# A fused multiply and GELU on one core: the first 4096 columns stored by the ACT queue while the last y load runs

## The chip, the cores, the metric

One core of one Trainium2 chip. The metric is the device time of one execution in microseconds (us); a median is given with its lowest and highest run. The kernels with no repeated timing (two, marked below) have one run each.

## The reference

```python
# x, y: float32, 1024 x 4096
z = x * y
out = 0.5 * z * (1 + tanh(sqrt(2 / pi) * (z + 0.044715 * z ** 3)))
```

Two arrays of 16.78 MB are read and one is written, 50.33 MB in all. Nothing is used twice.

## The kernel before

Each of the 128 partitions holds 8 rows of the matrix, that is 32768 columns of float32 (128 KB), contiguous in the main memory. x stays in a buffer of full size and is overwritten by the product and then by the result. y passes through a ring of half that size.

```python
X_LOADS = [(0, 16384), (16384, 32768)]
Y_LOADS = [(0, 16384, 0), (16384, 24576, 0), (24576, 32768, 8192)]   # from, to, place in the ring
STEP = 4096
STORES = [(0, 16384), (16384, 32768)]
# ... (set-up cut)
_hoist(nc, [load_x(0).ins, load_y(0).ins])       # issued at the very start, on SyncE
load_x(1)
for i in (1, 2):                                 # the ring must be free first
    nc.sync.wait_ge(sem_mul, (Y_LOADS[i][1] - Y_LOADS[1][0]) // STEP)
    load_y(i)

n = 0
for i, (a, b, r) in enumerate(Y_LOADS):
    # ... (wait for the x load of these columns, cut)
    nc.vector.wait_ge(sem_y[i], 16)
    for c in range(a, b, STEP):
        nc.vector.tensor_mul(...).then_inc(sem_mul, 1)          # xs = xs * ys
        n += 1
        nc.scalar.wait_ge(sem_mul, n)
        nc.scalar.activation(..., func=GELU).then_inc(sem_act, 1)   # xs = gelu(xs)

for i, (a, b) in enumerate(STORES):
    nc.sync.wait_ge(sem_act, b // STEP)
    nc.sync.dma_start(out=out_r[:, a:b], in_=xs[:, a:b]).then_inc(sem_o[i], 16)
for i in range(len(STORES)):
    nc.sync.wait_ge(sem_o[i], 16)
```

All transfers of the kernel are issued by SyncE, in this order: x0, y0, x1, y1, y2, store 0, store 1. "y2" is the last y load, "the last store" is that of columns 16384 to 32768.

## Time and profile before

| | before |
|---|---|
| time, first 3 runs | 121.03 us (120.79 to 121.08) |
| span of the profiled run | 119.5 us |
| VectorE, ScalarE busy | 35.0 us, 30.2 us |
| DMA engines busy | 98.5% of the span |
| last store: issued, then time to landing | 93.32 us, 26.1 us |

The page's groups give the length of one instruction (the number after the busy time, in ns), and the view of the tensor `out_dram` gives the time from issue to landing of its two stores.

```profile
L87 DVE TENSOR_TENSOR xs<-xs,ys 128x4096 f32<-128x4096 f32 x8 | 35.0, 4421 | 54.7 <-DMA ys<-in_y_dram 54.7
L94 ACT ACTIVATE xs<-xs 128x4096 f32<-128x4096 f32 x8 | 28.9, 3617 | 61.1 <-DVE xs L87 61.1
...
DMA to landing us min/median/max: 26.1/31.9/37.7
```

Both engines idle far longer than they work, and VectorE waits for nothing but y. The two stores are of the same size, yet one takes 26.1 and the other 37.7 us to land: the difference is time spent standing in the queue. The trace also has one record for each row that a DMA engine moves ("packet records" below); they are not a view of the page and are quoted as worked out from the trace. The records carry no engine number: 16 chains were put together by matching each start to the end before it, and each comes to the same 3.15 MB, but for a few of the smallest rows. The excess of a row is its duration less the median for its size. The "dip" is the mean excess per engine around the place where stores first follow loads.

### The profile page before, as it was taken

What the parts mean: (1) busy time and instruction counts of PE and PEld (TensorE: products, weight loads), DVE (VectorE), ACT (ScalarE), POOL (GpSimd) and SP (SyncE); (2) the same over time, 40 slices, a digit from 0 to 9 for tenths busy, and PEclk for the clock granted to TensorE, in tenths of its full rate; (3) what the DMA queues carried; (4) which work ended last, traced back from release to release, by engine and by line L of the source; (5) the groups of instructions that cost most, each with busy time, mean ns of one, the idle gap of its engine ahead of it and who ended that gap; (6) DMA issues with size and microseconds to landing.
All of it is one profiled execution on the core that took longest, in us unless ns stands there. A gap on an engine that the chain in (4) does not pass through costs nothing.

```text
span 119.5 us, 68 instructions
## 1 busy us (share of the span) xinstructions
DVE 35.0 (29%) x8; ACT 30.2 (25%) x9; POOL 0.2 (0%) x4
## 2 busy tenths in 40 slices
DVE  0000000000000199999600049959990000000000
ACT  3000000000000006797780000977479200000000
POOL 0000000000000000000000000000000000000000
DMA  9889888998899889988898989998899888988890
GB/s 351 351 373 680 351 351 351 636 417 351 351 636 417 351 351 526 526 351 351 351 526 351 504 373 482 395 526 351 351 395 658 351 351 351 702 351 351 351 680 22
DMA packets 1008, 50.33 MB, mean 421 GB/s; under 512 B 112, under 2 KB 112, under 8 KB 112
## 3 DMA queue, kind: packets, MB, share of 16 engines
q1 hardware_dynamic: 1008, 50.33, 98.5%
HBM read 33.55 MB, written 16.78 MB: 421 GB/s over the span
## 4 chain that ended last, share of the span: by engine, by line
DMA 53%; DVE 22%; ACT 3%; SPq 0%; issue 0%; DVEq 0%
DMA ys<-in_y_dram 53%; DVE xs L87 22%; ACT xs L94 3%; SPq L66 0%; DVEq L85 0%
## 5 line engine op out<-in xcount | busy, mean ns | idle before, releaser
L87 DVE TENSOR_TENSOR xs<-xs,ys 128x4096 f32<-128x4096 f32 x8 | 35.0, 4421 | 54.7 <-DMA ys<-in_y_dram 54.7
L94 ACT ACTIVATE xs<-xs 128x4096 f32<-128x4096 f32 x8 | 28.9, 3617 | 61.1 <-DVE xs L87 61.1
L94 ACT ACT_TABLE_LOAD x1 | 1.3, 1283 | 1.9 <-PEq L54 1.9
L120 POOL MEMSET const-bfloat16-1.0<- 128x1 bf16 x1 | 0.1, 102 | 0.0
L120 POOL MEMSET const-uint8-127<- 128x1 uint8 x1 | 0.1, 102 | 0.0
L120 POOL MEMSET const-float32-1.0<- 128x1 f32 x1 | 0.1, 99 | 0.0
L120 POOL MEMSET const-float32-0.0<- 128x1 f32 x1 | 0.1, 98 | 0.2 <-issue 0.2
## 6 DMA issues: line engine op xcount, KB each, us to landing
ys<-in_y_dram SPq DMA_DIRECT2D x2, 4096.0 KB, 21.1
xs<-in_x_dram SPq DMA_DIRECT2D x2, 40.3
out_dram<-xs SPq DMA_DIRECT2D x2, 31.9
ys<-in_y_dram SPq DMA_DIRECT2D x1, 40.8
```

The costliest lines, as they stand in the source:

```text
L87: nc.vector.tensor_mul(out=xs[:, c : c + STEP], in0=xs[:, c : c + STEP], in1=ys[:, r + c - a : r + c - a + STEP],).then_inc(sem_mul, 1)
L94: nc.scalar.activation(out=xs[:, c : c + STEP], in_=xs[:, c : c + STEP], func=GELU).then_inc(sem_act, 1)
L120: nc = _bacc.Bacc("TRN2", target_bir_lowering=False, num_devices=1)
```

## The change

The intent: begin to store before the loads are done, from a second queue, so that stores don't have to wait at the end of the line of loads.

```diff
-STORES = [(0, 16384), (16384, 32768)]
+STORES = [(0, 4096), (4096, 16384), (16384, 32768)]
...
+    def store(engine, i):
+        a, b = STORES[i]
+        engine.wait_ge(sem_act, b // STEP)
+        engine.dma_start(out=out_r[:, a:b], in_=xs[:, a:b]).then_inc(sem_o[i], 16)
...
             nc.scalar.wait_ge(sem_mul, n)
+            if c == Y_LOADS[1][0]:
+                store(nc.scalar, 0)
             nc.scalar.activation(
...
-    for i, (a, b) in enumerate(STORES):
-        nc.sync.wait_ge(sem_act, b // STEP)
-        nc.sync.dma_start(out=out_r[:, a:b], in_=xs[:, a:b]).then_inc(sem_o[i], 16)
+    store(nc.sync, 1)
+    store(nc.sync, 2)
```

## The prediction

> **What bounds the kernel now.** I read the page's head and its DMA rows first, because 33.55 MB in and 16.78 MB out with eight multiplies and eight activations looks like a copy with some arithmetic on the side.
>
> ```profile
> span 119.5 us, 68 instructions
> DVE 35.0 (29%) x8; ACT 30.2 (25%) x9; POOL 0.2 (0%) x4
> DMA  9889888998899889988898989998899888988890
> DMA packets 1008, 50.33 MB, mean 421 GB/s; under 512 B 112, under 2 KB 112, under 8 KB 112
> q1 hardware_dynamic: 1008, 50.33, 98.5%
> ```
>
> VectorE and ScalarE are busy under a third of the span; the 16 DMA engines are busy in every slice, 98.5% of the span, all on one queue. Next the chain of waits and the waits of the SyncE queue:
>
> ```profile
> DMA 53%; DVE 22%; ACT 3%; SPq 0%; issue 0%; DVEq 0%
> SPq L70 <- DVE xs L87: 56.2, 2, 47.9
> SPq L100 <- ACT xs L94: 33.8, 2, 30.5
> SPq L102 <- DMA out_dram<-xs: 25.8, 1, 25.8
> ```
>
> The chain ends at the issue of the second store and gives VectorE 22%. Taken literally it says that an earlier multiply would end the program earlier. That has to be checked against the time order, since a store that is issued may still stand in line:
>
> ```profile
> 58.80 0.33 SPq L70 DMA_DIRECT2D ys<-in_y_dram  x1
> 62.45 31.22 SPq L100 DMA_DIRECT2D out_dram<-xs  x2
> 74.92 3.62 ACT L94 ACTIVATE xs<-xs 128x4096 f32<-128x4096 f32 x1 [12.51 <-DVE xs L87]
> 80.88 8.76 DVE L87 TENSOR_TENSOR xs<-xs,ys 128x4096 f32<-128x4096 f32 x2 [1.66 <-DMA ys<-in_y_dram]
> 89.68 3.62 ACT L94 ACTIVATE xs<-xs 128x4096 f32<-128x4096 f32 x1 [0.72 <-DVE xs L87]
> ...
> 93.32 0.34 SPq L100 DMA_DIRECT2D out_dram<-xs  x1
> ```
>
> The first store is issued at 62.45 and the view of its tensor gives 37.7 us to landing, so it lands at 100.1, although 8.39 MB at 433 GB/s is only 19.4 us: it waits behind the y loads until about 80. The second is issued at 93.32, while the first is still moving; its data can start only at about 99.3. So it has 99.3 - 93.32 = 6.0 us of slack, about 5 after start-up latency (the first load of the program is issued at 0.00 and its first packet starts at 1.01). The 22% of VectorE is under cover of the queue. Stretches cut at these points:
>
> ```profile
> 60.00:76.80 16.80, 6.33 (x2) 4.29 (x2) 0.00 (x0) 1.00 0.98 425
> 76.80:80.00 3.20, 2.43 (x1) 2.48 (x2) 0.00 (x0) 1.00 1.07 369
> 80.00:99.30 19.30, 8.76 (x2) 10.11 (x3) 0.00 (x0) 1.00 0.99 431
> 99.30:118.50 19.20, 0.00 (x0) 0.00 (x0) 0.00 (x0) 1.00 1.00 433
> ```
>
> The columns end with the DMA share and GB/s. Loads alone reach 425, stores alone 431 to 433, and only 76.8 to 80.0, the last two rows of the last y load on each engine, dips to 369. The packet records of the trace (one record is one contiguous row of a partition) say the same per engine: the 640 packets of 64 KB have a median of 2.418 us, 27.1 GB/s, and the 256 of 32 KB 1.213 us. Fifteen of the 16 engines have no gap over 0.05 us between their first packet and the last. Each engine moves 3.146 MB, and 3.146 MB / 27.1 GB/s = 116.1 us. With 1.0 us before the first packet, 0.8 us more in that first packet, about 0.7 us in the dip, 0.2 us of slight slowing between 50 and 60, and some 0.5 us from the last packet to the end, this is 119.3 of the 119.5 us. The kernel is bound by bytes through the DMA engines, and all that a reordering can win back is the dip and what lies at the ends.
>
> **What the Trainium skill says.** First, the page "DMA: Bandwidth & Descriptors", section "Issuing engines are not separate DMA queues": transfers issued by ScalarE and SyncE end on the same 16 engines and interleave, and a second issuer saves only issue time. The issue rows here are 0.33 to 0.43 us each and hide behind a full queue, so there is nothing to save. Second, the same page, "Queues, rings and completion order": each engine goes round-robin between the rows that have work, at packet granularity. The trace of before has one queue only, so it can't confirm this. Third, "Where 436 GB/s comes from": 435 GB/s is given as the ceiling of the ports; the 433 GB/s of the last stretch agrees, and loads and stores reach the same figure here. Fourth, the page "Perfetto Trace Analysis", section "DMA Optimizations": loads on one issuing engine and stores on another may make sense. That is the change's intent; no run yet shows it.
>
> **The change part by part.**
> 1. Bytes: none added or removed. Rows of the first store go from one of 64 KB to one of 16 KB and one of 48 KB. From the two medians, fixed cost of a packet is 2 x 1.213 - 2.418 = 0.008 us. An engine has 8 partitions, so 8 x 0.008 = 0.064 us, and one more semaphore packet of 0.009 us: +0.07 us, on the path that sets the end.
> 2. ScalarE issues the small store once multiply 5 is done, at about 74.9. By the issue rows it costs it some 0.4 us, so the activation that starts at 74.92 starts near 75.3 and ends near 78.9. The next one starts at 79.26 because of multiply 6, so this delay is absorbed: 0.
> 3. The small store's data can start near 75.9 (issue to first packet 1.0 us). At that moment an engine is in its sixth y row of eight (75.63 to 76.84 on the engine that I followed), with two left. In turn with rows of 16 KB (estimate 0.61 us each by half of 1.213), they land about 2 x 0.61 = 1.2 us later: the last y load lands at 82.0 in place of 80.8.
> 4. The last two multiplies, the last activation and the second big store all move by this 1.2 us: issue at about 94.5, first data possible near 95.5. The bytes queued ahead of it are the same as before, so its turn comes at 99.3 + 0.07. Hidden, with almost 4 us left. Cost: 0.
> 5. The remaining five or six small rows alternate with 48 KB rows of the first SyncE store. The order changes, the sum doesn't.
> 6. The SyncE wait for a third store semaphore is satisfied long before the last one: 0.
>
> Sum: +0.07 us, plus or minus what the dip does.
>
> **The rivals.**
> *A bubble before the last store.* If the ScalarE row were served wholly ahead of the y rows, the y load would land 8 x 0.61 = 4.9 us later, at 85.7; 8.77 us of multiplies, 3.62 us of activation and 1.0 us of latency later the last store could start at 99.1. Its turn is at 99.3. Even this worst order just fits, and would cost 0 to 0.5 us: at most 121.6.
> *Switching between loads and stores costs.* The dip stands right before the one place where the program turns from loads to stores. If the turn causes it (0.7 us each), an alternation of two or three y rows with small rows makes three to five turns: +1.4 to +2.8 us, 122.4 to 123.8. Against it: the dip starts two rows before the turn, on all engines at the same time, which looks as much like a slow moment of the memory as a cost of the turn. One trace can't tell.
> *Loads and stores overlap.* If an engine could read for a store while it writes for a load, the 2.1 MB store would be partly free. Only the two or three y rows that remain can be its partners: at most about 2.4 us, 118.6. Against it: loads and stores both sit at the same 27.1 GB/s per engine, as if one common data path set it.
> *The dip goes.* If the second queue fills what stalls there, 0.7 us is won: 120.4.
>
> **Range and chances.** Center: 121.03 + 0.07 = 121.1 us. Before itself spread from 120.79 to 121.08. Down to 120.2 covers the dip gone and good luck; up to 122.2 covers one or two more turns. 2% is 2.42 us: faster needs full overlap of all that can overlap, 3%; slower needs nearly the full turn cost or a bubble that I don't see, 6%; within 2%, 91%.
>
> **What would show it.** A second DMA queue with about 2.1 MB on the page, and a DMA share near 98%; the wait of VectorE for the last y load longer by about 1.2 us than the 1.66 above; the last store issued near 94.5 with its time to landing down from 26.1 to about 25 us; a span of 119.6. Wrong it would be if the last store's time to landing fell to 20 to 21 us, issue to data without a queue (the bubble), if packet records in the mixed stretch were longer than their size explains (the turn), or if the rate between 76 and 80 rose well over 433 GB/s (overlap).

## The result, and the profile after

| | before | after |
|---|---|---|
| time, 6 runs each | 120.95 us (120.79 to 121.08) | 121.08 us (120.91 to 121.33) |
| span of the profiled run | 119.5 us | 120.0 us |

The ratio is 1.0013, with a 95% interval of 0.9999 to 1.0027: the same. A ratio here is the mean time of one kernel's fast runs over that of the other's of the same rounds, so it is not quite the ratio of the medians. The profiled run of after happened to be its slowest of six (121.33); the spans of the others lie between 119.6 and 119.9.

From the page of after, the head, the DMA queues (packets, MB, share of 16 engines) and the time to landing of the last store:

```profile
span 120.0 us, 70 instructions
q1 hardware_dynamic: 1008, 48.23, 94.2%
q10 hardware_dynamic: 144, 2.10, 4.1%
...
out_dram<-xs SPq DMA_DIRECT2D x1, 24.9
```

The second queue carries the 2.1 MB of the small store, and the shares add to 98.3%, against 98.5% on one queue before. The waits of the SyncE queue and the time order of after:

```profile
SPq L70 <- DVE xs L92: 56.2, 2, 47.9
SPq L77 <- ACT xs L101: 35.4, 2, 32.1
SPq L108 <- DMA out_dram<-xs: 24.6, 1, 24.6
```

```profile
74.85 0.37 ACTq L77 DMA_DIRECT2D out_dram<-xs  x1
75.27 3.62 ACT L101 ACTIVATE xs<-xs 128x4096 f32<-128x4096 f32 x1 [12.85 <-DVE xs L92]
79.19 3.62 ACT L101 ACTIVATE xs<-xs 128x4096 f32<-128x4096 f32 x1 [0.30 <-DVE xs L92]
82.52 8.76 DVE L92 TENSOR_TENSOR xs<-xs,ys 128x4096 f32<-128x4096 f32 x2 [3.37 <-DMA ys<-in_y_dram]
...
91.31 3.62 ACT L101 ACTIVATE xs<-xs 128x4096 f32<-128x4096 f32 x1 [0.72 <-DVE xs L92]
```

Reading them against before: the small store goes out at 74.85 and costs ScalarE 0.37 us; the next activation starts at 75.27 in place of 74.92, and the one after that still waits for VectorE, 0.30 us in place of 0.72. So the issue is absorbed. The last two multiplies start at 82.52 in place of 80.88, 1.64 us later. Everything behind them moves with them: SyncE waits 32.1 us for ScalarE in place of 30.5, and then 24.6 us for the last store in place of 25.8. What it waits more on one line it waits less on the next. The remainder of about 0.4 us is the difference between these two profiled spans, and the times of the other runs show less of it.

The packet records say where the small rows stood. On 15 of the 16 engines no small row went ahead of a row of y2, though the store had been issued some 5 us before. This is one of them:

```
start us  took us  size    queue
75.73     1.213    32 KB   SyncE   (y2)
76.94     1.556    32 KB   SyncE   (y2)
78.54     1.474    32 KB   SyncE   (y2, last row)
80.01     0.611    16 KB   ACT     (small store)
80.62     0.009    4 B     SyncE   (semaphore of y2)
80.62     0.611    16 KB   ACT
81.23     1.815    48 KB   SyncE   (next store)
83.04     0.611    16 KB   ACT
```

Each transfer ends with one record of 4 B on each engine; it is taken here for the one that raises the semaphore. The two last rows of y2 are slow (the dip, 0.98 us in the mean of the engines, 0.70 in before), then one small row goes ahead of the semaphore packet that tells VectorE of y2. On the sixteenth engine a small row went ahead of the last y2 row and another ahead of the semaphore, and this engine decided when y2 counted as landed. From 80 us on, rows of the two store queues alternate one to one, each with the duration that its size gives.

### The profile page after: what moved, and what is told of

It reads as the page before. It is cut to its first block, busy times and chain, and to the rows that moved or that the text cites. A ratio compares the mean times of both kernels' runs of the same rounds, so it can differ in the third digit from the quotient of the medians.

```text
span 120.0 us, 70 instructions
## 1 busy us (share of the span) xinstructions
DVE 35.0 (29%) x8; ACT 30.2 (25%) x9; POOL 0.2 (0%) x4
## 4 chain that ended last, share of the span: by engine, by line
DMA 54%; DVE 22%; ACT 3%; SPq 0%; issue 0%; DVEq 0%
DMA ys<-in_y_dram 54%; DVE xs L92 22%; ACT xs L101 3%; SPq L66 0%; DVEq L90 0%
## 6 DMA issues: line engine op xcount, KB each, us to landing
out_dram<-xs SPq DMA_DIRECT2D x1, 24.9
```

## The experiments

Twelve kernels ran, and all twelve gave correct results. Those of one group shared the runs of the kernel before.

### Group 1: the parts of the change

**early.** The small store is issued before ScalarE waits for multiply 5, so it meets the y loads with almost all their rows still to come.

```diff
+            if c == Y_LOADS[1][0]:
+                store(nc.scalar, 0)
             nc.scalar.wait_ge(sem_mul, n)
-            if c == Y_LOADS[1][0]:
-                store(nc.scalar, 0)
```

> The changed kernel, with the small store issued by ScalarE before it waits for multiply 5, so near 59 us: all its eight 16 KB rows per engine must then alternate with the y rows. Bytes theory: 121.1 us, small rows of 0.61 us between y rows of 1.21 us from about 61 to 75, the last y load lands 8 x 0.61 = 4.9 us later than in the kernel before (near 85.7), and the last store, issued near 98.2, just makes its turn at 99.4. Turn-cost theory (0.7 us for each change between load and store, some 16 of them): y lands near 97, and 121 + 11 = 132 us. Overlap theory (a store is free beside a load): up to 8 x 0.61 = 4.9 us less, 116 to 118 us.

Measured: 120.87 us (120.69 to 120.92, 6 runs) against 120.94 (11 runs), ratio 0.9991 [0.9978, 1.0005]. Its time order, with the stores:

```profile
58.77 0.38 ACTq L77 DMA_DIRECT2D out_dram<-xs  x1
62.41 36.03 SPq L77 DMA_DIRECT2D out_dram<-xs  x2
...
85.65 8.76 DVE L92 TENSOR_TENSOR xs<-xs,ys 128x4096 f32<-128x4096 f32 x2 [2.12 <-DMA ys<-in_y_dram]
```

y2 is ready at 85.65, 4.77 us later than in before; eight small rows of 0.61 us are 4.9. So a store row beside a load row costs its bytes, to about 0.1 us in 4.9. Overlap falls: nothing was free. The cost of each turn falls too: from 64 to 77 us small rows and y rows alternate and every one has its median duration. But one dip of 0.93 us is there, in the two y rows before the first small row, and none where y2 turns to the next store near 84.8 (excess 0.00).

**split_sp.** The rows are split as in the change, but the small store goes on SyncE, ahead of the next.

```diff
-            if c == Y_LOADS[1][0]:
-                store(nc.scalar, 0)
+    store(nc.sync, 0)       # after the loop, before store 1
     store(nc.sync, 1)
```

> The changed kernel with the small store put back on SyncE, ahead of the 48 KB-row store: the rows are split as in the change, but there is one queue. Bytes theory: 121.0 us (0.07 us over before), the last y load lands near 80.8 again and the last store is issued near 93.3. If the second queue itself costs something, this kernel is below the changed one by more than 0.2 us; if it is the split rows, it is as slow as the changed one.

Measured: 120.96 us (120.82 to 121.05), ratio 0.9999 [0.9986, 1.0011]. The small store is issued as soon as y2 is, 15.75 us sooner than in the change, and stands behind it:

```profile
59.10 0.44 SPq L77 DMA_DIRECT2D out_dram<-xs  x1
...
80.88 8.76 DVE L92 TENSOR_TENSOR xs<-xs,ys 128x4096 f32<-128x4096 f32 x2 [1.78 <-DMA ys<-in_y_dram]
```

The multiplies on y2 start at 80.88, exactly as before. So the second queue is what delays y2. The splitting of rows has no cost that these rounds can resolve, and the records give the same: 16 KB takes 0.611 and 48 KB 1.815 us, together 0.008 more than the 2.418 of 64 KB. That the changed kernel is slower than this one stays unresolved: 0.12 us between the medians of different rounds.

**whole.** ScalarE stores the whole first half at the same point, in 64 KB rows (STORES as before, its entry 0 issued by ScalarE, the other by SyncE).

```diff
-STORES = [(0, 4096), (4096, 16384), (16384, 32768)]
+STORES = [(0, 16384), (16384, 32768)]
...
     store(nc.sync, 1)
-    store(nc.sync, 2)
```

> The first half stored whole by ScalarE (64 KB rows), at the same point as the small store of the change. Bytes theory: 121.0 us. The engines have two y rows committed when it comes, so one 64 KB row goes ahead of the y semaphore on most engines (2.4 us) and on the slowest engine perhaps two: the last y load lands near 83.5 to 86, the last store is issued near 96 to 98.5, still in time for 99.4. If the slack of the last store is smaller than I think, the time rises above 121.5.

Measured: 121.16 us (120.88 to 121.8), ratio 1.0025 [1.0001, 1.0048].

```profile
83.65 8.76 DVE L92 TENSOR_TENSOR xs<-xs,ys 128x4096 f32<-128x4096 f32 x2 [4.44 <-DMA ys<-in_y_dram]
...
96.08 0.35 SPq L77 DMA_DIRECT2D out_dram<-xs  x1
```

The records show one 64 KB row (2.4 us) between the last y2 row and its semaphore on every engine. The landing is later by 2.77 us: 2.42 are the row that steps in front, and the dip of this profile was 1.02 us in place of 0.70. The last store, issued at 96.08, still gets its turn. The interval lets the kernel be a little slower than before, by 0.0 to 0.6 us; I have no cause for that.

**hold.** The kernel before, with the first store held until y2 has landed.

```diff
         nc.sync.wait_ge(sem_act, b // STEP)
+        if i == 0:
+            nc.sync.wait_ge(sem_y[2], 16)
```

> The kernel before, with the first store held until the last y load has landed: no store stands in the queue while the last y rows run. If the dip of the rate between 76.8 and 79 us comes from the turn (the engine reading ahead for the store), it is gone: y lands near 80.0, the store starts its data about 1.0 us after that (81.1 instead of 80.0): 120.95 + 1.1 - 0 = about 121.9 us. If the dip has to do with the place or time of those rows and not with the store, it stays at about 0.7 us, y lands at 80.8 and the store's data starts near 81.9: 122.8 us.

Measured: 121.66 us (121.51 to 121.8), ratio 1.0059 [1.0046, 1.0071].

```profile
80.08 0.35 SPq L102 DMA_DIRECT2D out_dram<-xs  x1
80.09 4.42 DVE L87 TENSOR_TENSOR xs<-xs,ys 128x4096 f32<-128x4096 f32 x1 [0.95 <-DMA ys<-in_y_dram]
```

The dip is gone (excess 0.01 us), y2 is ready at 80.09, 0.79 us sooner than in before, and in exchange the engines stand without data for 1.76 us in the mean. By the one trace of before this exchange is 1.76 less 0.70, or 1.06 us; the medians show 0.72. The dip differs from trace to trace (0.67 to 1.13 us below), and that of before is at the low end. So the dip belongs to a store that stands behind the loads. It is not a slow moment of the memory.

### Group 2: the dip, and the slack of the last store

**still** (one run). Multiplies 5 and 6 are held until y2 has landed, so nothing computes beside its last rows.

```diff
         nc.vector.wait_ge(sem_y[i], 16)
+        if i == 1:
+            nc.vector.wait_ge(sem_y[2], 16)
```

> The kernel before, with multiplies 5 and 6 held until the last y load has landed, so that VectorE and ScalarE are idle from 62.4 to about 80. If the dip between 76.8 and 79 us comes from the engines' traffic in the on-chip memory beside the load, it is gone and y lands near 80.1; if not, the dip of 0.7 us stays. Either way multiplies 5 to 8 then take 17.5 us, the last activation ends near 102, the last store's data starts near 103 instead of 99.4: about 124.5 us. That also measures what a late last store costs.

Measured: 124.48 us. The dip stays (1.10 us), so computation beside the load does not cause it. The last store's data starts near 103.2, and the delay is paid for in full.

**turn** (one run). The first store is issued between the two last y loads.

```diff
         nc.sync.wait_ge(sem_mul, (Y_LOADS[i][1] - Y_LOADS[1][0]) // STEP)
+        if i == 2:
+            store(0)
         load_y(i)
```

> The kernel before, with the first store issued between the two last y loads on the same queue, so the turn from loads to stores comes near 69.7 us, after the first of them, and the last y load lands near 99.4. If the dip belongs to the turn, it is found in the last rows of the first y load, near 67 to 69 us, and not at the end of the last y load. If it belongs to the rows (the last columns of y), it moves with them to about 96 to 98 us. If it belongs to the computation beside it, it is found where VectorE and ScalarE run together (near 75 to 79). The last store then starts about 8.8 + 3.6 + 1 = 13.5 us late: near 134 us.

Measured: 135.02 us.

```profile
71.30 8.76 DVE L94 TENSOR_TENSOR xs<-xs,ys 128x4096 f32<-128x4096 f32 x2 [12.60 <-DMA ys<-in_y_dram]
...
100.40 8.76 DVE L94 TENSOR_TENSOR xs<-xs,ys 128x4096 f32<-128x4096 f32 x2 [20.34 <-DMA ys<-in_y_dram]
...
112.83 0.34 SPq L77 DMA_DIRECT2D out_dram<-xs  x1
```

The dip (0.95 us) moved to the end of the first of the two y loads, between 66 and 70 us, which is why its multiplies start at 71.30 and not at 70.47. The last rows of y2 are clean. The dip goes with the turn, not with the columns and not with the time. The store's early place made 8.39 MB go ahead of y2, and with the last store not ready the engines idled 14.2 us in the mean.

**pad1, pad2.** One or two dummy activations after the last, which the last store must wait for.

```diff
+    for k in range(2):                      # pad1: range(1)
+        c = k * STEP
+        nc.scalar.activation(
+            out=ys[:, c : c + STEP], in_=ys[:, c : c + STEP], func=GELU
+        ).then_inc(sem_act, 1)
     for i, (a, b) in enumerate(STORES):
-        nc.sync.wait_ge(sem_act, b // STEP)
+        nc.sync.wait_ge(sem_act, b // STEP + 2 * i)     # pad1: + 1 * i
```

> The kernel before, with one dummy activation of 3.62 us after the last, and the last store waits for it: issued near 96.9 instead of 93.3, data possible near 98, its turn is at 99.3. If the chain's 22% of VectorE lay on the path, the time would rise by 3.6 us to 124.6; by the bytes theory it stays at 121.0.

> The same with two dummy activations: issued near 100.6, data from 101.6, against a turn at 99.3: a bubble of 2.3 us, 123.3 us. With the 3.6 us of slack gone in the first dummy, this second one is paid for by more than half.

Measured: pad1 120.88 us (120.78 to 120.98), ratio 0.9995 [0.9977, 1.0012]; pad2 122.75 us (122.45 to 122.92), ratio 1.0145 [1.0128, 1.0163]. In pad2 the store is issued late:

```profile
93.47 7.10 ACT L100 ACTIVATE ys<-ys 128x4096 f32<-128x4096 f32 x2
100.60 0.34 SPq L106 DMA_DIRECT2D out_dram<-xs  x1
```

In pad1 the last store is issued near 96.8 and still takes longer to land than the 19.4 us that its bytes need, so it stood in line:

```profile
L106 SPq DMA_DIRECT2D out_dram<-xs x2: 343/346/348, 62.4 to 96.8; - x2
...
DMA to landing us min/median/max: 22.6/30.1/37.7
```

The first 3.6 us cost nothing, the second 1.8 us. This is the direct proof that the last store of the kernel before has slack, and that the chain of waits, which ends at its issue, named work that was not on the path. I had expected 123.3 for pad2; its dip was 1.13 us in the profiled run, so the queue reached the last store near 99.8 instead of 99.3, and the gap was 1.75 us in the mean of the engines in place of 2.3.

### Group 3: is it the first store of a program?

**warm, warm_mid.** A tiny store of zeros into columns 0 to 128, overwritten later, issued by ScalarE at the start (warm) or after multiply 1 (warm_mid). The first large store waits for it.

```diff
+    nc.vector.memset(warm, 0.0).then_inc(sem_z, 1)
+    nc.scalar.wait_ge(sem_z, 1)             # warm_mid: in the loop, where n == 1
+    nc.scalar.dma_start(out=out_r[:, 0:128], in_=warm).then_inc(sem_w, 16)
```

> The kernel before, with a tiny store (128 rows of 512 B of zeros, overwritten later) issued by ScalarE at the start, near 2.5 us, while the first loads run. In the runs so far the dip of about 0.7 to 1.0 us stood only before the first store row of a program that came right behind loads, and not before later turns. If the first store of a program pays it once, whatever its size, the dip moves to about 3 to 5 us and the end of the last y load is smooth: y lands near 80.1; the time is 120.9 if the cost is the same there and 120.2 if the start-up hides it. If a dip belongs to the first turn to a large store, it stays near 77 to 79 and the time is 120.95 to 121.1.

> The same tiny store, issued by ScalarE after multiply 1 near 45.8 us, in the middle of the second x load. First-store theory: a dip of 0.7 to 1.0 us near 46 to 50 us and none near 77: 120.95 us. Large-turn theory: none or little near 46 to 50, the dip stays near 77: 121.0 us. If the tiny store passes without a dip and the dip near 77 is gone too, the time is 120.2 us and this version beats both kernels.

Measured: warm 121.15 us (120.95 to 121.43), ratio 1.0019 [0.9999, 1.0039]; warm_mid 121.04 us (120.86 to 121.23), ratio 1.0006 [0.9988, 1.0023]. The tiny rows of 512 B slip between the x rows in both with no excess beside them over 0.02 us, and the dip near 77 us stays, 0.87 and 0.67 us. So the dip isn't paid by whichever store comes first.

### Group 4: one turn or each turn, and a version that avoids it

**two_turns.** The small store on SyncE between the two last y loads: one queue, two turns from loads to stores.

```diff
         load_y(i)
+        if i == 1:
+            store(nc.sync, 0)
...
-            if c == Y_LOADS[1][0]:
-                store(nc.scalar, 0)
```

> The changed kernel with its small store on SyncE between the two last y loads: one queue, with two turns from loads to stores, near 69.6 and near 84 us, with 9.7 us of y rows between them. If each turn from loads to stores costs about 0.8 us, there are two dips (67 to 70 and 81 to 84) and the time is 121.8 us; if only the first one does, as in the early kernel, there is one dip near 67 to 70 and the time is 121.0. The last y load lands near 85.7, the last store is issued near 98.2 and still makes its turn near 99.4.

Measured: 121.11 us (120.89 to 121.28, 5 runs) against 120.87 (11 runs), ratio 1.0015 [1.0003, 1.0027].

```profile
71.18 8.76 DVE L94 TENSOR_TENSOR xs<-xs,ys 128x4096 f32<-128x4096 f32 x2 [12.41 <-DMA ys<-in_y_dram]
...
85.92 8.76 DVE L94 TENSOR_TENSOR xs<-xs,ys 128x4096 f32<-128x4096 f32 x2 [5.97 <-DMA ys<-in_y_dram]
```

One dip of 0.72 us before the first turn, and 0.06 us at the second. Only the first turn to a store of large rows is dear, with one queue as with two. The interval lets this kernel be slower than before by 0.04 to 0.33 us; no run shows why.

**late_turn.** The last y load is cut into 6656 and 1536 columns. The first store waits for the larger part, so that it reaches the engines when the last small y rows end.

```diff
-Y_LOADS = [(0, 16384, 0), (16384, 24576, 0), (24576, 32768, 8192)]
+Y_LOADS = [(0, 16384, 0), (16384, 24576, 0), (24576, 31232, 8192), (31232, 32768, 14848)]
+Y_ENDS = [16384, 24576, 32768]
...
         load_y(i)
+    load_y(3)
...
         for c in range(a, b, STEP):         # a, b now from Y_ENDS
+            if c + STEP > Y_LOADS[3][0]:
+                nc.vector.wait_ge(sem_y[3], 16)
...
         nc.sync.wait_ge(sem_act, b // STEP)
+        if i == 0:
+            nc.sync.wait_ge(sem_y[2], 16)
```

> An attempt to win the dip back: the last y load is cut into 6656 and 1536 columns, and the first store is issued only when the larger part has landed, so that it reaches the engines (0.9 us after its issue) about when the small part's last rows end. In the hold kernel there was no dip, but 1.8 us without data. If the dip is the store meeting loads that have two rows or more still to come, it is gone or small here and there is no gap: 120.3 us. If the dip comes with any contact of the store with loads in flight, it stays: 121.0 us. If the landing comes later than I think, a gap of some tenths opens instead.

Measured: 120.17 us (120.04 to 120.54, 6 runs) against 120.87, ratio 0.9942 [0.9928, 0.9955].

```profile
span 118.9 us, 70 instructions
q1 hardware_dynamic: 1152, 50.33, 98.4%
...
70.42 17.43 DVE L92 TENSOR_TENSOR xs<-xs,ys 128x4096 f32<-128x4096 f32 x4 [11.63 <-DMA ys<-in_y_dram]
...
78.42 13.45 SPq L107 DMA_DIRECT2D out_dram<-xs  x2
```

The store, issued at 78.42, starts its rows between 79.27 and 79.84, right behind the last y rows. The dip is 0.05 us, the mean time without data under 0.1 us, and VectorE runs its last four multiplies without a break. The gain of 0.7 us is of the size of the dip, 0.67 to 1.13 us in the traces that turn where before does. The smaller last y rows are a second difference; hold, with the rows of before, shows that the late store alone removes the dip. This version is 0.6% below before in shared rounds, clear of the noise; the changed kernel was timed in other rounds (121.08).

## Why the prediction was right

The forecast was 121.1 us with 91% for "within 2%"; the result is 121.08. That the two are 0.02 us apart is partly luck: the median of before moved from 121.03 (3 runs) to 120.95 (6 runs), and the interval of the ratio stands for a change of -0.01 to +0.33 us, where +0.07 was forecast. What was right is the account of why nothing large could change.

- **The bound** held. pad1 shows the slack of the last store, early shows that moving 2.1 MB of stores among the loads changes nothing in the sum, and the DMA share stayed at 98.3%. "Busy in every slice" is a misreading of one digit: the last slice shows 0. No sum rests on it.
- **Step 1, +0.07 us for more rows**: the 0.008 us per row is confirmed by the new sizes. The sum is too small for the times to show.
- **Step 2** was right: the activation started at 75.27 (75.3 forecast), and the delay was absorbed.
- **Step 3** was right in size by a mechanism that was only half so. I let two small rows go "in turn with" the two y rows that were left, from 75.9 on, 1.2 us. On most engines the two y rows ran first; one small row then went ahead of y2's semaphore. Only the engine that came last had two small rows ahead of its semaphore. Measured were 1.64 us: two rows are 1.22, and the rest of about 0.4 goes with the dip, which was 0.28 us larger in the mean in this profile. On the engines that came last it was 1.23 us in place of 0.74, and these rows had begun 0.07 us sooner: 1.22 + 0.49 - 0.07 = 1.64. That the dip was larger is not shown to be the change's doing: among the kernels that run like before up to that point it was 0.67 to 1.13 us.
- **Step 4** was right: the last store was issued near 95.0 (94.5 forecast), landed 24.9 us later (25), and cost nothing. Even whole, with the issue at 96.08, was at most 0.6 us slower.
- **The rivals.** Overlap is refuted by early. The bubble is real when the store is late by more than its slack (pad2, still), and the change didn't reach it. The turn was mis-sized: I charged 0.7 us to each of three to five turns; it comes once (early, two_turns). My objection to it, that a dip in rows before the turn looks like a slow moment of the memory, is refuted by hold and turn. "The dip goes" did not come true in the changed kernel, and did in late_turn, where nothing of the second queue is needed.

What stays open: why only the first turn costs, and why a tiny store doesn't count as one. The runs fix when the dip comes (large store rows standing behind loads for the first time) and when it doesn't (a store that arrives as the loads end, a second turn, rows of 512 B). They do not show what happens in the engine.

## What to carry to other kernels

In this kernel the DMA engines were busy for 98% of the span, and as long as an order kept them so (after, early, split_sp, pad1), it moved who waits and not the end; one that let them idle paid for it (turn, 14 us). With engines so full, look for rows that take longer than their size before looking for a better order. The chain of waits ends at the issue of a transfer, so check whether that transfer could have started at once: a time to landing well over bytes divided by rate (26.1 us against 19.4) meant here that it stood in line and that the chain before it had slack (pad1). A store put on a second queue beside a load delayed the load's semaphore by whole rows (0.61 us each in after, 2.4 us in whole), so keep those rows small if someone waits for the load.

## What the Trainium skill lacked or had wrong

- "DMA: Bandwidth & Descriptors", section "Queues, rings and completion order", gives round-robin between queues by packets of typically 9 to 17 descriptors. The round-robin is seen here (after, early), but its turns were of one row of a partition, 0.611 us of 16 KB and 1.815 us of 48 KB. The page also doesn't say how long a new queue waits for its first turn: the small store, issued at 74.85, began at 79.3 to 80.6, where a store that met idle engines began 0.85 to 1.0 us after its issue (hold). That it waits for rows already taken up fits this and is not shown.
- The same section doesn't say that a row of another queue can go between a transfer's last row and its semaphore packet. It delayed a landing by 0.61 us a row of 16 KB and by 2.4 us a row of 64 KB (whole).
- The same page, "Where 436 GB/s comes from", says that for transfers between the main memory and the on-chip one the memory's share of about 358 GB/s binds. This program on one core ran at 27.1 GB/s per engine, 433 GB/s over 16, for loads and stores alike, near the port ceiling of 435 that it also gives. The sentence does not say that it is for two cores at once; the same passage calls a measured 425 GB/s near the rate of the fabric.
- "Perfetto Trace Analysis", section "DMA Optimizations", says that loads and stores on different issuing engines may make sense, and does not say when it brings nothing. With the DMA engines full it gave a ratio of 1.0013 (after) and 0.9991 (early), no gain. The other page, as the prediction cites it, has this right: a second issuer saves only the time of issue, and here that was hidden.
- No page that I read has the cost of the first turn from loads to large stores: 0.67 to 1.13 us in the mean of the engines, once in each program here, gone at 0.05 us when the store arrives as the loads end (late_turn).
